# Hymba block on one core: the recursion keys turned on VectorE, one small-matmul cluster for the last Gram chunk, norms and bonus sums, and a place for each store

## The chip, the core and the metric

The kernel runs on one core of one Trainium2 chip. The metric is the device time of one execution in microseconds, as the median of several runs.

## What is computed

One layer over 512 tokens plus 16 prepended meta tokens, model width 2048, all in fp32 to the outside:

```python
hn = rmsnorm(h_res, norm_in_g)            # h_res: 16 meta tokens + 512 tokens, width 2048
P = hn @ w_in                             # 8320 columns: r, k, v, g (1024 each), 2 x 64 low rank; B, C, h, gc (1024 each)
# branch A: 16 heads of 64, RWKV-7 (r, k, v, g after a token shift)
a     = sigmoid(a0 + al @ a_lora_up); decay = exp(-exp(w_raw))
kk    = (k * k_k) / max(norm_per_head(k * k_k), 1e-12);  k = k * (1 + (a - 1) * k_a)
for t in frames:                          # state S is 64 x 64 for each head
    S = S * decay_t - (S @ kk_t) outer (kk_t * a_t) + v_t outer k_t
    y_t = S @ r_t
y_a = (groupnorm(y) + sum_per_head(r * k * r_k) * v) * silu(g)
# branch B: short gated convolution
y_b = B * causal_conv3(C * h) * silu(gc)
h_res = h_res + concat(y_a, y_b) @ w_out
out = rmsnorm(h_res)[:, 16:]
```

## The kernel before

**The projections.** The input projection is cut into 65 column tiles of 128 columns with 16 steps along the width. Each step is three matmuls in a split form of fp32: high weight x high input, high x low, low x high (L315, operands `wh`/`wl` and `xh`/`xl`). Weights arrive in transfers of 512 KB (`wr`, three buffers) and are split into a high part on ScalarE (L126) and a low part by subtraction on VectorE or POOL (L127). The tiles are named by what they give: `ps_k`, `ps_r`, `ps_v`, `ps_g`, then `ps_C`, `ps_h`, `ps_B`, `ps_gc` for the convolution. Evacuation from PSUM is on VectorE (L334); L352, L362 and L405 finish the gates and the convolution. The output projection (L1070) has the same form.

**The recurrence** is done in nine chunks of 64 frames for eight pairs of heads. `prepare(i)` builds what a pair needs, and after every second pair `invert` builds the triangular inverses of both; afterwards `recur` runs the chunks in order for all pairs. The inner matmuls are fp32, 64 rows high.

For one pair, `prepare` first makes elementwise products (`ar`, `bk`, squares `sq_h`/`sq_l`, bonus products `rk_h`/`rk_l`). TensorE then runs three clusters of its own: the *Gram cluster* (L625, chunks 0 to 7, masked into `gt` on VectorE by L635); the *second Gram cluster*, which holds chunk 8 (four records of L625) and 16 transposes of the keys (L655) that ScalarE copies into `bt` (L661, two); and the *norm cluster* (L666 and L667 the squared norms, two pieces of 288 columns each in high and low parts; L670 and L671 the bonus sums `zb`). Behind these come stores to DRAM scratch `sn` and `sg`, the stashes into the per-pair operand area `opd` (`ar`, `gt`, `bt`, `vs`, `xT`), loads `d` and `nd`, and the small block inverse on VectorE (L701 to L734; L719 and L728 are its products, whose operands have steps of 16 elements, L725 and L734 the sums; the result is `y`). `y` is stored to `sx`, loaded back in transposed places into `xT` (`load_inverse`), and `invert` goes on from there: `xn` on VectorE (L785), matmuls from L792 on, and the stash of `xT`. `recur` loads chunk operands `ct` from `opd` (L870) and runs L889 (`rz`), L906 (`u`) and the state update and outputs (L939 `zs`, L943 `zy`).

**The order of work.** TensorE's order is written by hand. The projection is a generator; `fill(ns)` draws that many ns of projection matmuls between two clusters, and `until(key)` draws until a tile is done. The table `FW` names these amounts, in ns of projection work. `later(ns, fn)` issues a DMA once that much more projection has been drawn; `run_pending` flushes what is due. All loads and stores go through SyncE's queue in program order; `tc.issue_after(state["dma"])` puts a transfer behind the latest weight load. The other engines' orders come from a scheduler with priorities; `ahead()` raises the priority of what it holds.

```python
FW = dict(
    evac=34, start=1062, lora=2200, gram=8000, gram_b=13500, gram2=4800, gram3=3500, misc=2000, v=2000, vt=1000, solve=22500, ...
...
        fill(FW["gram2"])          # second Gram cluster: chunk 8, key transposes
        fill(FW["gram3"])          # norm cluster: norms, bonus sums
        fill(FW["misc"])           # stores, block inverse
```

Of the kernel before, what the change touches and what calls it, by code (L numbers as in the profile page):

```python
# [18 lines left out]
P = 128  # L19
DM = 2048  # L20
KT = DM // P
SEQ = 512
# [18 lines left out]


FW = dict(
    evac=34, start=1062, lora=2200, gram=8000, gram_b=13500, gram2=4800, gram3=3500, misc=2000, v=2000, vt=1000, solve=22500, solve_first=26000,
    tr=3200, lev=3000, cp=4200, out=1500, begin=17000, p=2900, u=2900, s=5200, last=3700, mix=2600,
)

# [29 lines left out]
def hymba_kernel(ctx: ExitStack, tc: tile.TileContext, xt, xtok, w_in, w_out, pv, lup, cst, msk, gf, out):  # L77
# [299 lines left out]
    def use(what, i, ps):  # L377
        if what == "lora":
            use_lora(ps)
        elif what in ("k", "v"):  # L380
            t = cq.tile([P, LP], F32, tag=what, name=f"{what}{i}")
            nc.gpsimd.memset(t[:, META:CH], 0.0)
            shift_full(ps, tile_of[what] + i, f"{what}{i}", padded(t))
            got[what, i] = t
        elif what in ("r", "g"):
            t = cq.tile([P, SEQ], F32, tag=f"r{i % 2}" if what == "r" else "g", name=f"{what}{i}")
            shift_real(ps, tile_of[what] + i, f"{what}{i}", t)
            if what == "g":
                gate(t, f"r{i}")
                later(6000, lambda: nc.sync.dma_start(gated[i], t))  # L390
            got[what, i] = t
        elif what == "C":
            u = tm(f"u{i}")
            scaled(TAIL, ps, u, 14)
            got[what, i] = u
        elif what == "h":
            u = got["C", i]
            hh = tm(f"hh{i}")
            scaled(TAIL, ps, hh, 14)
            n = SEQ + 2  # L400
# [81 lines left out]
    def later(ns, fn):  # L482
        pending.append((clock[0] + ns, fn))
        pending.sort(key=lambda e: e[0])
# [81 lines left out]
    def stash(i, src, o, n, row=0, rows_n=P, c0=0, cn=NCH, step=1):  # L566
        nc.sync.dma_start(spot(i, row, rows_n, c0, cn, step, o, n), src)

    def prepare(i):
        p = i % 2  # L570
        until("k", i)
# [49 lines left out]
        bt = cq.tile([P, 2, NCH - 1, CH], F32, tag="bt", name=f"bt{i}")  # L621

        def gram(z, c, c0):
            for h, hs, ho in heads:
                nc.tensor.matmul(  # L625
# [21 lines left out]
        masked(za, 0, 4)  # L647
        masked(zc, 4, 8)
        fill(FW["gram2"])
        ze = [pi.tile([P, 1, P], F32, tag=("misc", "ser")[h], name=f"g{i}_8_{h}") for h in range(2)]  # L650
        zz = [pz.tile([P, NCH - 1, CH], F32, tag="tz", name=f"bt{i}_{h}") for h in range(2)]
        gram(ze, 8, 8)
        for c in range(NCH - 1):
            for h, hs, ho in heads:
                nc.tensor.transpose(  # L655
                    zz[h][:, c], bk[hs, c, h : h + 2, :].rearrange("p a s -> p (a s)"),
                    ident[hs, 64 * h : 64 * h + 64],
                )
        masked(ze, 8, 9)
        for h in range(2):  # L660
            nc.scalar.copy(bt[:, h], zz[h])  # L661
        fill(FW["gram3"])
        n2 = tr(f"n2{i}")
        for j, (a, b) in enumerate(((0, 288), (288, LP))):
            z = pi.tile([2, b - a], F32, tag=("misc", "ser")[j], name=f"n2_{i}_{a}")
            nc.tensor.matmul(z, ones[:, P : P + 2], sqh[:, a:b], start=True, stop=False)  # L666
            nc.tensor.matmul(z, ones[:, P : P + 2], sql[:, a:b], start=False, stop=True)  # L667
            nc.scalar.copy(n2[0:2, a:b], z)
        zb = pz.tile([P, SEQ], F32, tag="tz", name=f"zb{i}")
        nc.tensor.matmul(zb, ones[:, 0:P], rh, start=True, stop=False)  # L670
# [14 lines left out]
        nc.sync.dma_start(  # L685
            bass.AP(tensor=sn.tensor, offset=sn.offset, ap=[[CH, 2], [P, NCH], [1, CH]]), c3(n2[0:2])
        )
        for h in range(2):
            nc.sync.dma_start(rows(sg, h), gt[64 * h : 64 * h + 64, h, :, 0:CH])
        NB = 8 * NCH  # L690
        d = cq.tile([NB, 256], F32, tag="d", name=f"d{i}").rearrange("p (s t) -> p s t", t=16)
        stash(i, ar.rearrange("p c a s -> p c (a s)"), O_AR, 2 * CH)
        for h, hs, ho in heads:
            stash(i, gt[ho, h], O_KK, 2 * CH, 64 * h, 64)
            stash(i, gt[hs, h, :, CH:P], O_BR, CH, 64 * h, 64)
        nd = cq.tile([NB, 16], F32, tag="nd", name=f"nd{i}")
        nc.sync.dma_start(d, blocks(sg))
        nc.sync.dma_start(nd, sn.rearrange("(p s) -> p s", s=16))
        y = cq.tile([NB, 256], F32, tag="y", name=f"y{i}").rearrange("p (s t) -> p s t", t=16)
        nc.gpsimd.memset(y, 0.0)  # L700
        nc.vector.tensor_scalar(out=nd, in0=nd, scalar1=1e-24, scalar2=None, op0=ALU.max)  # L701
# [56 lines left out]
        nc.sync.dma_start(rbd[i], r)  # L758
        fill(FW["v"])

        vs = cq.tile([P, NCH, CH], F32, tag="vs", name=f"vs{i}")
        nc.vector.transpose(vs.rearrange("p c s -> p (c s)"), v)
        for b in range(4):
            for t in range(2):
                stash(
                    i, vs[32 * b : 32 * b + 32, :, 32 * t : 32 * t + 32], O_V + 32 * (b % 2), 32,
                    64 * (1 - b // 2) + 32 * t, 32,
                )
        fill(FW["vt"])
# [2 lines left out]
    def invert(two):  # L772
# [85 lines left out]
        for t in two:  # L858
            if t["i"] % 2 == 0:
                stash(t["i"], t["xT"], O_X, CH)  # L860
            else:
                for h, hs, ho in heads:
                    stash(t["i"], t["xT"][hs], O_X, CH, 64 - 64 * h, 64)
        fill(FW["out"] if first < NPAIR - 2 else FW["begin"])

    def load_chunk(ch, c, pairs, ops):
# [8 lines left out]
    def recur(ch):  # L875
# [4 lines left out]
        for c in range(NCH):  # L880
# [54 lines left out]
            for n in range(max(len(here), len(there))):  # L935
                if n < len(here):
                    d, j, t, o, x, a, b = here[n]
                    for h, hs, ho in heads:
                        nc.tensor.matmul(d[hs, j], t[hs, o : o + CH], x[hs], start=(a == 0), stop=(a == b - 1))  # L939
                if n < len(there):  # L940
                    d, j, x, o, t, a, b = there[n]
                    for h, hs, ho in heads:
                        nc.tensor.matmul(d[ho, j], t[hs, o : o + CH], x[hs], start=(a == 0), stop=(a == b - 1))  # L943
# [51 lines left out]
    for i in range(0, NPAIR, 2):  # L995
        invert([prepare(i), prepare(i + 1)])
    until("g", NPAIR - 1)
    ph2.close()
    with tc.tile_pool(name="ch", bufs=1, side="right", reuse_waits="tile") as ch:
        recur(ch)  # L1000
# [34 lines left out]
    for j in range(NPAIR + 4, KT):  # L1035
        while ("gc", j - NPAIR) not in ready:
            step()
        split_mix(j)
    for _ in flow:
        pass  # L1040
# [194 lines left out]
```

## Time and profile before

| | |
|---|---|
| median of 3 runs | 1056.24 us (1056.13 to 1057.02) |
| the profiled execution | 1054.6 us |
| its span, first to last instruction | 1052.8 us |
| TensorE busy | 1034.8 us (98%) |
| VectorE busy | 566.4 us (54%) |
| ScalarE, POOL busy | 365.9 us (35%), 308.3 us (29%) |
| granted TensorE clock, mean | 0.996 |

The profile is of one execution. Its rows give the start, the duration, the engine, the line, the operation with its tiles (output, then inputs), and in brackets the idle time before it with what ended that. In rows of groups, three numbers behind the count are the least, the median and the greatest duration in ns. Matmuls are pipelined: neighbours overlap, so the distance between starts is what one costs. A `x4` behind a row means that four records of one line, tile and form are drawn together.

### The profile page before, as it was taken

The page shows a single profiled execution, that of the slowest core. Times are in us where ns is not written, and L with a number is a line of the kernel's source. Part 1 is how long each engine was busy: PE and PEld are TensorE (multiplying, and loading weights), DVE is VectorE, ACT ScalarE, POOL GpSimd, SP SyncE. Part 2 cuts the span into 40 slices and gives each one's busy share as a digit, 9 for nine tenths or more (in the row PEclk, how much of TensorE's full clock was granted, in tenths as well). Part 3 has the DMA queues.
Part 4 walks back from the last instruction along what each step waited for, and adds up shares of the span by engine and source line. Part 5 has one row for each costly group of instructions (what it writes and reads, how often), then busy time and mean ns, then how long its engine had stood idle before and what let it go on. Part 6 is the DMA issues. An engine that isn't in the chain of part 4 may idle for free.

```text
span 1052.8 us, 23986 instructions
## 1 busy us (share of the span) xinstructions
PE 1034.8 (98%) x9973; PEld 945.1 (90%) x9973; DVE 566.4 (54%) x1072; ACT 365.9 (35%) x682; POOL 308.3 (29%) x315
## 2 busy tenths in 40 slices
PE   7999999999999999999999999999999999999996
PEld 6999998999998999989999989888898988888885
DVE  6774965559563658653757642455454781212132
ACT  7543422433332433233443232222222342323232
POOL 0132413324222323132323231323233242424232
PEclk9999999999999999999999999999999999999999
DMA  8446475364854363753364748778654978322314
GB/s 297 135 124 155 121 175 142 108 153 120 197 152 115 108 164 112 175 155 114 104 170 127 178 129 291 232 214 248 181 146 112 275 233 302 98 87 95 100 61 160
DMA packets 182893, 167.49 MB, mean 159 GB/s; under 512 B 120960, under 2 KB 143232, under 8 KB 182400
## 3 DMA queue, kind: packets, MB, share of 16 engines
q1 hardware_dynamic: 182208, 164.90, 53.7%
q8 instruction: 78, 1.28, 0.5%
q10 hardware_dynamic: 576, 1.07, 0.3%
q14 instruction: 31, 0.25, 0.1%
HBM read 129.05 MB, written 36.88 MB: 158 GB/s over the span
## 4 chain that ended last, share of the span: by engine, by line
PE 90%; DVE 4%; issue 2%; DMA 1%; ACT 1%; POOL 1%; SPq 0%; DVEq 0%; ACTq 0%; POOLq 0%
PE o L1070 17%; PE ps_g L315 9%; PE ps_gc L315 9%; PE ps_k L315 9%; PE ps_B L315 8%; PE ps_h L315 8%; PE ps_C L315 8%; PE ps_r L315 7%; PE ps_v L315 7%; PE g L625 2%; PE zs L939 1%; PE ps_lora L315 1%; PE rz L889 1%; PE zy L943 1%; DMA wq<-in_w_in_dram 1%
## 5 line engine op out<-in xcount | busy, mean ns | idle before, releaser
L127 POOL TENSOR_TENSOR wl<-wr,wh 128x512 fp32r<-128x512 f32 x150 | 211.2, 1410 | 456.2 <-ACT wh L126 423.2
L126 ACT CAST wh<-wr 128x512 fp32r<-128x512 f32 x312 | 188.7, 619 | 385.2 <-PE o L1070 92.2
L127 DVE TENSOR_TENSOR wl<-wr,wh 128x512 fp32r<-128x512 f32 x162 | 124.8, 775 | 241.4 <-ACT wh L126 236.0
L1070 PE MATMUL o<-wh,m 128*128 128x512 f32 (+1 forms) x484 | 145.3, 384 | 0.0
L1070 PEld LDWEIGHTS o<-wh,m 128*128 128x128 f32 x484 | 89.6, 188 | 21.3
L1070 PE MATMUL o<-wl,m 128*128 128x512 f32 (+1 forms) x242 | 92.6, 389 | 0.0
L315 PE MATMUL ps_k<-xl,wh 128*128 128x264 f32 x256 | 73.2, 286 | 0.0
L315 PE MATMUL ps_g<-xh,wl 128*128 128x258 f32 (+1 forms) x256 | 72.2, 282 | 0.9 <-DVE wl L127 0.8
L315 PE MATMUL ps_v<-xh,wh 128*128 128x264 f32 x256 | 73.1, 286 | 0.0
L315 PE MATMUL ps_k<-xh,wh 128*128 128x264 f32 x256 | 73.0, 285 | 0.0
L315 PE MATMUL ps_r<-xh,wh 128*128 128x258 f32 (+1 forms) x256 | 72.2, 282 | 0.7 <-ACT wh L225 0.7
L315 PE MATMUL ps_h<-xh,wl 128*128 128x258 f32 (+1 forms) x256 | 72.8, 285 | 0.0
L315 PE MATMUL ps_k<-xh,wl 128*128 128x264 f32 x256 | 72.7, 284 | 0.0
L315 PE MATMUL ps_v<-xh,wl 128*128 128x264 f32 x256 | 72.7, 284 | 0.0
L315 PE MATMUL ps_v<-xl,wh 128*128 128x264 f32 x256 | 72.7, 284 | 0.0
L315 PE MATMUL ps_g<-xl,wh 128*128 128x258 f32 (+1 forms) x256 | 72.4, 283 | 0.0
L315 PE MATMUL ps_h<-xh,wh 128*128 128x258 f32 (+1 forms) x256 | 72.3, 282 | 0.0
L315 PE MATMUL ps_g<-xh,wh 128*128 128x258 f32 (+1 forms) x256 | 72.3, 282 | 0.0
L315 PE MATMUL ps_C<-xh,wh 128*128 128x258 f32 (+1 forms) x256 | 72.3, 282 | 0.0
L315 PE MATMUL ps_C<-xh,wl 128*128 128x258 f32 (+1 forms) x256 | 72.3, 282 | 0.0
L315 PE MATMUL ps_r<-xl,wh 128*128 128x258 f32 (+1 forms) x256 | 72.1, 282 | 0.0
L315 PE MATMUL ps_h<-xl,wh 128*128 128x258 f32 (+1 forms) x256 | 72.1, 282 | 0.0
(271 smaller groups left out, 2705.9 us busy)
## 6 DMA issues: line engine op xcount, KB each, us to landing
wr<-in_w_in_dram SPq DMA_DIRECT2D x127, 512.0 KB
ct<-opd SPq DMA_DIRECT2D x64, 288.0 KB
wr<-in_w_out_dram SPq DMA_DIRECT2D x32, 512.0 KB
opd<-ar SPq DMA_DIRECT2D x8, 576.0 KB
opd<-gt SPq DMA_DIRECT2D x16, 288.0 KB
opd<-bt SPq DMA_DIRECT2D x32, 128.0 KB
xres<-in_xtok_dram SPq DMA_DIRECT2D x4, 768.0 KB
out_dram<-xres SPq DMA_DIRECT2D x6, 512.0 KB
```

Of the source, the lines that this page charges most:

```text
L126: nc.scalar.copy(hi, rq)
L127: eng.tensor_tensor(out=lo, in0=rq, in1=hi.bitcast(F32), op=ALU.subtract)
L315: nc.tensor.matmul(ps[r], ww[:, w], xx[:, kt, a:b], start=(kt == 0 and n == 0), stop=(kt == KT - 1 and n == 2))
L625: nc.tensor.matmul(z[h][:, c - c0], bk[hs, c, h : h + 2, :].rearrange("p a s -> p (a s)"), ar[hs, c].rearrange("p a s -> p (a s)"), start= ...
L889: nc.tensor.matmul(z[e][ho if e else hs, 0, k], t[hs, o : o + CH], t[hs, O_V : O_V + CH] if part else st[hs, 4 * e + k], start=(part == 0 ...
L939: nc.tensor.matmul(d[hs, j], t[hs, o : o + CH], x[hs], start=(a == 0), stop=(a == b - 1))
L943: nc.tensor.matmul(d[ho, j], t[hs, o : o + CH], x[hs], start=(a == 0), stop=(a == b - 1))
L1070: nc.tensor.matmul(ps[t + p], mm[:, tk], ww[:, o], start=(jj == 0 and q == 0), stop=(jj == KT - 1 and q == 2))
```

## The change

- The 16 TensorE transposes of a pair's keys and ScalarE's two copies are gone. Two VectorE transposes of 32x32 blocks (in place of L655 and L661) write `bt` instead, in a layout in which the keys of B and K alternate element by element; the stash puts it so into `opd`, in eight smaller transfers in place of four, and `recur` reads its stationary operand of `zs` with a step of two elements.
- The norm cluster's matmuls move into the second Gram cluster. The norms are cut into 512 and 64 columns in place of 288 and 288; the 64 lie in spare columns of the Gram tile. `gram3` is gone, `gram2` becomes 5500.
- Each store gets a place in the run of projection work: `sn`, `sg`, `d` and `nd` behind the latest weight load, all stashes and the stores of `rbd` and `mixd` by `later` with distances of their own, the gate's store at 14000 in place of 6000, and for odd pairs `sx` and `load_inverse` at 20500 and 22500 in place of 13500 and 16500. The stash of the inverse comes 5500 later. `run_pending` is called at two more places.

```diff
-    ... gram2=4800, gram3=3500, misc=2000, ...
+    ... gram2=5500, misc=2000, ...
-                later(6000, lambda: nc.sync.dma_start(gated[i], t))
+                later(14000, lambda: nc.sync.dma_start(gated[i], t))
-            nc.sync.dma_start(mixd[8 + i], cv)
+            later(9000, lambda: nc.sync.dma_start(mixd[8 + i], cv))
+    def behind(dst, src):
+        with tc.issue_after(state["dma"]):
+            nc.sync.dma_start(dst, src)
+    def stash_later(ns, *a):
+        later(ns, lambda: stash(*a))
...
         fill(FW["gram2"])
-        ze = [pi.tile([P, 1, P], F32, tag=("misc", "ser")[h], name=f"g{i}_8_{h}") for h in range(2)]
-        zz = [pz.tile([P, NCH - 1, CH], F32, tag="tz", name=f"bt{i}_{h}") for h in range(2)]
-        gram(ze, 8, 8)
-        for c in range(NCH - 1):
-            for h, hs, ho in heads:
-                nc.tensor.transpose(
-                    zz[h][:, c], bk[hs, c, h : h + 2, :].rearrange("p a s -> p (a s)"),
-                    ident[hs, 64 * h : 64 * h + 64],
-                )
-        masked(ze, 8, 9)
-        for h in range(2):
-            nc.scalar.copy(bt[:, h], zz[h])
-        fill(FW["gram3"])
+        ze = [pz.tile([P, P + CH], F32, tag="tz", name=f"g{i}_8_{h}") for h in range(2)]
+        gram([z[:, 0:P].unsqueeze(1) for z in ze], 8, 8)
         n2 = tr(f"n2{i}")
-        for j, (a, b) in enumerate(((0, 288), (288, LP))):
-            z = pi.tile([2, b - a], F32, tag=("misc", "ser")[j], name=f"n2_{i}_{a}")
+        zn = pi.tile([2, SEQ], F32, tag="misc", name=f"n2_{i}")
+        zs = ((zn, 0, SEQ), (ze[0][0:2, P : P + CH], SEQ, LP))
+        for z, a, b in zs:
             nc.tensor.matmul(z, ones[:, P : P + 2], sqh[:, a:b], start=True, stop=False)
             nc.tensor.matmul(z, ones[:, P : P + 2], sql[:, a:b], start=False, stop=True)
-            nc.scalar.copy(n2[0:2, a:b], z)
-        zb = pz.tile([P, SEQ], F32, tag="tz", name=f"zb{i}")
+        zb = pi.tile([P, SEQ], F32, tag="ser", name=f"zb{i}")
         ...
+        with ahead():
+            for z, a, b in zs:
+                nc.scalar.copy(n2[0:2, a:b], z)
+            masked([z[:, 0:P].unsqueeze(1) for z in ze], 8, 9)
         nc.scalar.copy(r, zb)
         fill(FW["misc"])
+        bt = cq.tile([P, NCH - 1, 2, CH // 2, 2], F32, tag="bt", name=f"bt{i}")
+        for a in range(2):
+            nc.vector.transpose(bt[:, :, :, :, a], bk[:, 0 : NCH - 1, a].rearrange("p c (t s) -> p c t s", t=2))
...
-        later(13500 if p else 29000, lambda: nc.sync.dma_start(blocks(sx), y))
-        later(16500 if p else 33000, load_inverse)
+        later(20500 if p else 29000, lambda: nc.sync.dma_start(blocks(sx), y))
+        later(22500 if p else 33000, load_inverse)
         for h, hs, ho in heads:
-            stash(i, bt[hs, h], O_B, CH, 64 * h, 64, 0, NCH - 1)
-            stash(i, bt[ho, h], O_K, CH, 64 * h, 64, 0, NCH - 1)
+            for b in range(2):
+                for t in range(2):
+                    stash_later(
+                        6500 + 1000 * (4 * h + 2 * b + t), i, bt[64 * h + 32 * b : 64 * h + 32 * b + 32, :, t].rearrange("p c s a -> p c (s a)"),
+                        O_B + 64 * b, 64, 64 * h + 32 * t, 32, 0, NCH - 1,
+                    )
...
-                        here += [(zs, j, t, O_B, u[:, e, k], 0, 2), (zs, j, t, O_K, t[:, O_V : O_V + CH], 1, 2)]
+                        bb = t[:, O_B : O_B + 2 * CH].rearrange("p (s a) -> p a s", a=2)
+                        here += [(zs, j, bb[:, 0], 0, u[:, e, k], 0, 2), (zs, j, bb[:, 1], 0, t[:, O_V : O_V + CH], 1, 2)]
```

The other stores are turned in the same manner: `ar` at 1500, `gt` at 2500 to 5500, `rbd` at 12500, `vs` at 14000 to 21000, the stash of the inverse at 5500.

More of the change, by code (lines that the diff above doesn't have):

```diff
@@ L43 @@
 FW = dict(
-    evac=34, start=1062, lora=2200, gram=8000, gram_b=13500, gram2=4800, gram3=3500, misc=2000, v=2000, vt=1000, solve=22500, solve_first=26000,
+    evac=34, start=1062, lora=2200, gram=8000, gram_b=13500, gram2=5500, misc=2000, v=2000, vt=1000, solve=22500, solve_first=26000,
     tr=3200, lev=3000, cp=4200, out=1500, begin=17000, p=2900, u=2900, s=5200, last=3700, mix=2600,
@@ L683, in blocks @@
             return bass.AP(tensor=t.tensor, offset=t.offset, ap=[[BLK, 8 * NCH], [CH, 16], [1, 16]])
-        nc.sync.dma_start(
+        behind(
             bass.AP(tensor=sn.tensor, offset=sn.offset, ap=[[CH, 2], [P, NCH], [1, CH]]), c3(n2[0:2])
@@ L688, in prepare @@
         for h in range(2):
-            nc.sync.dma_start(rows(sg, h), gt[64 * h : 64 * h + 64, h, :, 0:CH])
+            behind(rows(sg, h), gt[64 * h : 64 * h + 64, h, :, 0:CH])
         NB = 8 * NCH
         d = cq.tile([NB, 256], F32, tag="d", name=f"d{i}").rearrange("p (s t) -> p s t", t=16)
-        stash(i, ar.rearrange("p c a s -> p c (a s)"), O_AR, 2 * CH)
+        stash_later(1500, i, ar.rearrange("p c a s -> p c (a s)"), O_AR, 2 * CH)
         for h, hs, ho in heads:
-            stash(i, gt[ho, h], O_KK, 2 * CH, 64 * h, 64)
-            stash(i, gt[hs, h, :, CH:P], O_BR, CH, 64 * h, 64)
+            stash_later(2500 + 1000 * h, i, gt[ho, h], O_KK, 2 * CH, 64 * h, 64)
+            stash_later(4500 + 1000 * h, i, gt[hs, h, :, CH:P], O_BR, CH, 64 * h, 64)
         nd = cq.tile([NB, 16], F32, tag="nd", name=f"nd{i}")
-        nc.sync.dma_start(d, blocks(sg))
-        nc.sync.dma_start(nd, sn.rearrange("(p s) -> p s", s=16))
+        behind(d, blocks(sg))
+        behind(nd, sn.rearrange("(p s) -> p s", s=16))
         y = cq.tile([NB, 256], F32, tag="y", name=f"y{i}").rearrange("p (s t) -> p s t", t=16)
@@ L757, in prepare @@
         nc.vector.tensor_tensor(out=r, in0=r, in1=v[:, CH:LP], op=ALU.mult)
-        nc.sync.dma_start(rbd[i], r)
+        later(12500, lambda: nc.sync.dma_start(rbd[i], r))
         fill(FW["v"])
@@ L764, in prepare @@
             for t in range(2):
-                stash(
-                    i, vs[32 * b : 32 * b + 32, :, 32 * t : 32 * t + 32], O_V + 32 * (b % 2), 32,
+                stash_later(
+                    14000 + 1000 * (2 * b + t), i, vs[32 * b : 32 * b + 32, :, 32 * t : 32 * t + 32], O_V + 32 * (b % 2), 32,
                     64 * (1 - b // 2) + 32 * t, 32,
@@ L857, in invert, with put_inverse @@
                     nc.vector.tensor_copy(two[q]["xT"][lo, 2 - e : NCH : 2, 32:CH], z[e][lo, q])
[L858 to L863, printed above, removed]
+        def put_inverse():
+            for t in two:
+                if t["i"] % 2 == 0:
+                    stash(t["i"], t["xT"], O_X, CH)
+                else:
+                    for h, hs, ho in heads:
+                        stash(t["i"], t["xT"][hs], O_X, CH, 64 - 64 * h, 64)
+        later(5500, put_inverse)
         fill(FW["out"] if first < NPAIR - 2 else FW["begin"])
@@ L938, in recur @@
                     for h, hs, ho in heads:
-                        nc.tensor.matmul(d[hs, j], t[hs, o : o + CH], x[hs], start=(a == 0), stop=(a == b - 1))
+                        w = t[hs, o : o + CH] if o else t[hs]
+                        nc.tensor.matmul(d[hs, j], w, x[hs], start=(a == 0), stop=(a == b - 1))
                 if n < len(there):
@@ L997, in hymba_kernel @@
     until("g", NPAIR - 1)
+    run_pending(float("inf"))
     ph2.close()
@@ L1037, in hymba_kernel @@
             step()
+        run_pending(float("inf"))
         split_mix(j)
```

1 line of the change is left out of this document (removed).

## The prediction

> **What bounds the kernel now.** I read the page's busy shares and chain first, then TensorE's own waits, then timelines around the two small clusters that the change touches.
>
> ```profile
> PE 1034.8 (98%) x9973; PEld 945.1 (90%) x9973; DVE 566.4 (54%) x1072; ACT 365.9 (35%) x682; POOL 308.3 (29%) x315
> PE 90%; DVE 4%; issue 2%; DMA 1%; ACT 1%; POOL 1%; SPq 0%; DVEq 0%; ACTq 0%; POOLq 0%
> PE rz L939 <- issue: 1.6, 1, 1.6
> PE zy L943 <- issue: 1.0, 1, 1.0
> PE ps_B L315 <- DVE wl L127: 0.9, 1, 0.9
> PE ps_g L315 <- DVE wl L127: 0.8, 2, 0.4
> ```
>
> TensorE is busy for 98% of the span and carries 90% of the chain that ended last. Its waits are few and short. So the time moves only with the work in TensorE's stream, with the waits named here, and with waits that the change creates. VectorE, ScalarE and SyncE count only where one of them makes TensorE late.
>
> **Part 1: the clusters.** For each of the eight pairs the matmuls change in two places. This is the second Gram cluster of pair 0, then its norms and bonus sums:
>
> ```profile
> 82.34 0.28 PE L315 MATMUL ps_r<-xh,wh 128*128 128x258 f32 x1
> 82.55 0.49 PE L625 MATMUL g<-ar,bk 64*128 64x128 f32 x4
> 82.88 0.66 PE L655 MATMUL bt<-cs,bk 64*128 64x64 f32 x16
> 83.47 0.38 PE L315 MATMUL ps_r<-xl,wh 128*128 128x258 f32 x1
> ...
> 87.24 0.28 PE L315 MATMUL ps_r<-xh,wl 128*128 128x258 f32 x1
> 87.36 0.29 PE L666 MATMUL n<-sq_h,ones 128*2 128x288 f32 x1
> 87.88 0.40 PE L670 MATMUL zb<-rk_h,ones 128*128 128x512 f32 x1
> 88.35 0.28 PE L315 MATMUL ps_r<-xh,wh 128*128 128x256 f32 x1
> ```
>
> Matmuls overlap, so I use distances between starts. A projection matmul of this width takes 0.12 us (87.24 to 87.36). The one at 82.34 therefore ends its slot at 82.46, and the projection resumes at 83.47: the second Gram cluster costs 1.01 us. Of that, 0.09 is the change into the 64-row shape, 0.33 the four Gram records (82.55 to 82.88), and 0.59 the 16 key transposes with the way out. The norms, four matmuls of 288 columns, take 87.36 to 87.88, 0.13 each; a 512-column bonus matmul takes 0.235 ((88.35 - 87.88)/2). That makes 0.99, with no cost on the way in or out. Before: 2.00 us for a pair.
>
> After: the entry 0.09, the four records 0.33, and a way out which these rows do not separate from the transposes; 0 to 0.09 by the way in, I take 0.04. Then the norms in another cut: two of 512 columns at 0.235, two of 64 columns. No row has a 64-column matmul at full height. By width it would be 0.03 (0.13 x 64/288); the whole 0.13 is the ceiling. The weight load of this form gives a value between:
>
> ```profile
> L667 PEld LDWEIGHTS n<-sq_l,ones x16: 82/83/83, 87.4 to 577.5; 128*2 128x2 f32 x16
> ```
>
> I take 0.08, because a load of 83 ns must fit in front of each. With the bonus sums, 2 x 0.235, the cluster is 0.46 + 0.47 + 0.16 + 0.47 = 1.56 us (1.42 to 1.71). It saves 0.44 for a pair (0.29 to 0.58), and eight pairs **3.5 us (2.3 to 4.6)**. The Trainium skill ("TensorEngine Tiling (Array Packing)", Key Properties) says that changing the tiling mode drains TensorE; the 0.09 agrees in kind, and since the four Gram records remain, this change keeps that switch.
>
> **Part 2: waits that go.** In each of the groups of pairs 2/3, 4/5 and 6/7 TensorE stops once as a g tile begins:
>
> ```profile
> 255.97 0.28 PE L315 MATMUL ps_g<-xl,wh 128*128 128x258 f32 x1
> 256.64 0.39 PE L315 MATMUL ps_g<-xh,wl 128*128 128x258 f32 x1 [0.39 <-DVE wl L127]
> ...
> 408.75 0.28 PE L315 MATMUL ps_g<-xl,wh 128*128 128x258 f32 x1
> 409.41 0.39 PE L315 MATMUL ps_g<-xh,wl 128*128 128x258 f32 x1 [0.38 <-DVE wl L127]
> ...
> 561.72 0.28 PE L315 MATMUL ps_g<-xl,wh 128*128 128x258 f32 x1
> 562.14 0.39 PE L315 MATMUL ps_g<-xh,wl 128*128 128x258 f32 x1
> ...
> 254.71 0.68 DVE L734 TENSOR_REDUCE y<-prod 72x64 f32<-72x512 f32 x1
> 255.31 0.68 DVE L552 TENSOR_TENSOR rk_l<-r,rk_h 128x512 fp32r<-128x512 f32 x1
> 255.91 1.28 DVE L127 TENSOR_TENSOR wl<-wr,wh 128x512 fp32r<-128x512 f32 x2
> ```
>
> Start distances less 0.12 give 0.55, 0.54 and 0.30 us, 1.4 in all. VectorE is the reason: its weight subtraction (L127) stands behind the end of the previous pair's inverse (L734) and behind rk_l. After the change that inverse comes earlier, because the projection drawn between the second cluster and the stores shrinks from 4800 + 3500 + 2000 to 5500 + 2000 ns, 2.8 us less. The instruction order of the built kernel also has this subtraction ahead of the end of the inverse, of rk_l and of the key transposes. I count **1.4 us saved (0 to 1.4)**; what is late next there is the evacuation of the v tiles, which TensorE needs only once the next tile of that buffer begins.
>
> **Part 3: a wait that comes.** In the first group (pairs 0 and 1) VectorE's order changes for the worse. Before:
>
> ```profile
> 158.10 0.39 PE L315 MATMUL ps_B<-xl,wh 128*128 128x512 f32 x1
> 159.43 0.50 PE L315 MATMUL ps_B<-xh,wl 128*128 128x512 f32 x1 [0.94 <-DVE wl L127]
> ...
> 164.63 0.40 PE L315 MATMUL ps_gc<-xh,wh 128*128 128x512 f32 x1
> 165.10 0.40 PE L315 MATMUL ps_gc<-xh,wl 128*128 128x512 f32 x1
> ...
> 164.48 0.69 DVE L127 TENSOR_TENSOR wl<-wr,wh 128x512 fp32r<-128x512 f32 x1 [1.72 <-ACT wh L126]
> 165.09 0.68 DVE L334 TENSOR_TENSOR b<-ps_B,rs 128x512 f32<-128x512 f32 x1
> 165.69 0.70 DVE L785 STREAM_TRANSPOSE xn<-xT 128x512 f32<-128x512 f32 x1
> ```
>
> The first gc matmuls need the low halves at 165.10, 0.47 us after gc begins, and L127 made them in time. After the change b's evacuation (L334, which cannot start before the B tile ends where gc starts) stands ahead of that L127. Then b takes 0.60 (165.09 to 165.69) and L127 0.69, against 0.47: 0.8, and 0.15 for the handovers, about **0.95 us** of new wait. L127 is not always that quick: at the stop behind 158.10 two of them took 3.47 us, 1.74 each, which I put down to POOL's share of the same work running beside them.
>
> ```profile
> 157.59 3.47 DVE L127 TENSOR_TENSOR wl<-wr,wh 128x512 fp32r<-128x512 f32 x2
> ```
>
> By that the new wait would be 0.60 + 1.74 - 0.47, near 2 us. The old stop (159.43 - 158.10 - 0.235 = 1.1) stays, and may change: the same subtraction now stands behind the last steps of the inverse; I take 0.2 (-0.3 to 1). The inverse of this group is reached sooner after gc begins, since the pairs' own work moved forward against the projection, so its first transpose of x (xn, 0.70) stands behind one more subtraction: I take 0.35 (0 to 0.7). Together **1.5 us lost (0 to 4)**.
>
> **Part 4: what I count at nothing.** *Key transposes on VectorE*: two of 128x512 for a pair at the 0.70 of the xn row, 11 us in all on an engine with 46% idle. They write every second element; if that costs as in the rows below, 1.1 each and 18 us. They stand behind the weight subtractions that are due at that point. The place with the least cover is pair 2, where the first of them is ahead of ar:
>
> ```profile
> 211.42 0.69 DVE L607 TENSOR_TENSOR ar<-r,e 128x512 f32<-128x512 f32 x1
> 213.04 0.71 PE L625 MATMUL g<-ar,bk 64*128 64x128 f32 x8
> ```
>
> ar is done at 212.11, 0.93 before the Gram cluster; 0.70 fits, 1.1 makes a wait of 0.2. *ScalarE* loses two copies a pair. *Stores*: SyncE's blocking ar store waits no longer in the run of weight loads, which only adds slack to them; the eight smaller key stores replace four. *Inverse*: odd pairs load it later (22500 in place of 16500), while its use comes nearer, so its cover shrinks. By the constants and the order of the built kernel I estimate 6 to 7 us of projection between its new place and its use (L792 before), where there were 13; no row names this load as a wait of TensorE now, and I hold what is left enough. *Recursion*: the state update's stationary operand now takes every second element. The trace of before has no such load. I take nothing, bounds below.
>
> **Sum.** -3.5 - 1.4 + 1.5 = -3.4 us on 1054.6 us of the profiled execution (span 1052.8): 1051.2. The median of runs is 1056.24, 1.6 above it; the same step gives **1052.8**.
>
> **Rivals.**
> *(a) The strided weight loads slow the recursion: slower than before.*
>
> ```profile
> L939 PEld LDWEIGHTS zs<-ct x256: 135/135/135, 657.7 to 780.8; 64*64 64x64 f32 x128
> 659.43 0.28 PE L939 MATMUL zs<-ct 64*64 64x64 f32 x4
> 659.65 0.38 PE L315 MATMUL ps_h<-xh,wl 128*128 128x256 f32 x1
> L719 DVE TENSOR_TENSOR prod<-d,y x56: 156/166/1071, 101.8 to 595.9; 72x8 f32<-72x8 f32 x32, 72x64 f32<-72x64 f32 x16, 72x512 f32<-72x512 f32 x8
> L725 DVE TENSOR_REDUCE tt<-prod x56: 115/158/684, 102.0 to 597.0; 72x4 f32<-72x8 f32 x32, 72x16 f32<-72x64 f32 x16, 72x64 f32<-72x512 f32 x8
> ```
>
> The zs matmuls of the first chunk run from 657.6 to 659.65, 2.0 us for 64 with a load each. The nearest row with a step is L719, whose operand steps by 16 elements: 1.07 us where a contiguous read of the same size (L725) takes 0.68, 1.57 times as long. If the loads stretch like that and TensorE with them, eight chunks lose 8 x 2.0 x 0.57 = 9 us, up to 16 at twice. With the rest: 1062 (to 1069). It decides from 0.2 us a chunk on. For it: the loads (135 ns) are as long as the matmuls allow. Against it: the nearest strided row has a step eight times as large, and is on another engine. The Trainium skill ("SBUF — State Buffer", Door 1: The DMA port swizzle) says that SBUF is read in 16-byte lines, and that two hits on a line are enough for full speed: a step of two fp32 gives two, so by it the loads cost nothing, while L719's step gives one hit per line and pays, as its row shows. But the same sentence has each crossing to a new line pay, and this operand crosses twice as many. Chance 0.11.
>
> *(b) New waits eat the gain.* A slow L127 makes part 3 cost 3 to 4, pair 2's Gram cluster and a late inverse load add 0.2 to 1: no change, 1055 to 1057. For it: VectorE's order in the first group has no slack at all. Against it: only one of four groups has that order. Chance 0.19.
>
> *(c) The order costs nothing*, because the subtraction gets ahead: -3.5 - 1.4 = -4.9, 1051.3, on the forecast's side.
>
> **How the numbers follow.** Forecast with (c) 0.70, (b) 0.19, (a) 0.11. About 0.2% (2.1 us) is what a measurement of this kernel can tell. All of the first lies beyond it on the fast side; of (b) 0.17 is within it and 0.02 above: faster 0.70, same 0.17, slower 0.13. Low end: -4.6 - 1.4 gives 1050.2, and 0.7 less if one of the recursion's stops for issue (1.6 and 1.0 in the waits) shrinks: 1049.5. High end: 1057.5, (b) with its worst terms; (a) is left out.
>
> **What would show it.** Right: no L655, a merged cluster of about 1.5 us; no ps_g wait on L127; a wait of gc on L127 in the first group near 160 us; zs clusters still near 2.0 us in the first chunk. Wrong: zs loads over 135 ns, key transposes over 1.1 us, TensorE waiting on ar, on xn or on a chunk load.

## The result, and the profile after

The changed kernel takes 1050.93 us (median of 4 runs, 1050.09 to 1051.21) against 1056.18 for the kernel before (4 runs, 1055.93 to 1057.02): ratio 0.995, 95% interval 0.9934 to 0.9966. The profiled execution is 1051.02 us (span 1049.2), where the one before was 1054.6 (span 1052.8): 3.6 us between the two profiles, 5.25 between the medians. The forecast was 1052.8.

The page of the changed kernel, shares of busy time and the chain that ended last:

```profile
PE 1031.6 (98%) x9845; PEld 940.8 (90%) x9845; DVE 580.1 (55%) x1088; ACT 360.0 (34%) x666; POOL 311.1 (30%) x315
...
PE 94%; DMA 2%; issue 1%; DVE 1%; POOL 0%; SPq 0%; ACT 0%; DVEq 0%; ACTq 0%; POOLq 0%
```

TensorE has 128 instructions and 3.2 us of busy time less, and still bounds the kernel. Its waits (line, releaser, us in total, times, longest):

```profile
PE ps_B L315 <- DVE wl L127: 1.6, 1, 1.6
PE ps_lora L315 <- DVE xl L190: 1.5, 3, 1.0
...
PE ps_gc L315 <- DVE wl L127: 0.9, 1, 0.9
...
PE ps_h L315 <- issue: 0.6, 1, 0.6
PE t L801 <- DVE xn L794: 0.5, 1, 0.5
PE rz L902 <- DMA ct<-opd: 0.5, 1, 0.5
PE zy L958 <- issue: 0.2, 1, 0.2
```

The ps_g rows are gone. ps_B has grown, and three waits are new: gc on the subtraction, the inverse's first matmuls on xn, and the recursion's first matmuls on a chunk load. The merged cluster of pair 0 in TensorE's timeline:

```profile
83.89 0.28 PE L315 MATMUL ps_r<-xh,wh 128*128 128x258 f32 x1
84.10 0.49 PE L631 MATMUL g<-ar,bk 64*128 64x128 f32 x4
84.52 0.40 PE L663 MATMUL n<-sq_h,ones 128*2 128x512 f32 x1
84.75 0.39 PE L664 MATMUL n<-sq_l,ones 128*2 128x512 f32 x1
84.98 0.19 PE L663 MATMUL g<-sq_h,ones 128*2 128x64 f32 x1
85.01 0.19 PE L664 MATMUL g<-sq_l,ones 128*2 128x64 f32 x1
85.04 0.48 PE L666 MATMUL zb<-rk_h,ones 128*128 128x512 f32 x1
85.36 0.40 PE L667 MATMUL zb<-rk_l,ones 128*128 128x512 f32 x1
85.59 0.28 PE L315 MATMUL ps_r<-xl,wh 128*128 128x258 f32 x1
```

From the end of the slot at 84.01 to 85.59 it costs 1.58 us. The two pieces of 64 columns take 0.03 each, so the pair of them costs 0.06; the first bonus matmul takes 0.32 in place of 0.235. Its weight load of 0.19 us begins 0.03 ahead of it (85.01), where in the kernel before it began 0.13 ahead (87.75 and 87.88). I take that for the reason; it was not tested.

The first group, TensorE and then VectorE:

```profile
165.25 0.39 PE L315 MATMUL ps_gc<-xl,wh 128*128 128x512 f32 x1
166.56 0.50 PE L315 MATMUL ps_gc<-xh,wl 128*128 128x512 f32 x1 [0.92 <-DVE wl L127]
...
167.68 0.69 PE L801 MATMUL t<-xn,gt 64*64 64x64 f32 x32
168.88 0.52 PE L801 MATMUL t<-xn,gt 64*64 64x64 f32 x20 [0.50 <-DVE xn L794]
...
156.54 1.54 DVE L405 SCALAR_TENSOR_TENSOR cv<-u,pvt,cv 128x512 f32<-128x512 f32 x2 [1.25 <-ACT cv L403]
158.00 1.76 DVE L127 TENSOR_TENSOR wl<-wr,wh 128x512 fp32r<-128x512 f32 x1
165.21 0.69 DVE L334 TENSOR_TENSOR b<-ps_B,rs 128x512 f32<-128x512 f32 x1 [5.46 <-PE ps_B L315]
165.82 2.38 DVE L127 TENSOR_TENSOR wl<-wr,wh 128x512 fp32r<-128x512 f32 x2
168.12 0.70 DVE L794 STREAM_TRANSPOSE xn<-xT 128x512 f32<-128x512 f32 x1
```

VectorE is idle for 5.46 us ahead of b, then does b, the two subtractions and xn in a row while TensorE waits for the second and the fourth of them. That is the order that the prediction read from the built kernel.

### The profile page after: what moved, and what is told of

The parts are those of the page before. It is cut to its first block, busy times and chain, and to the rows that moved or that the text cites. A ratio compares the mean times of both kernels' runs of the same rounds, so it can differ in the third digit from the quotient of the medians.

```text
span 1049.2 us, 23744 instructions
## 1 busy us (share of the span) xinstructions
PE 1031.6 (98%) x9845; PEld 940.8 (90%) x9845; DVE 580.1 (55%) x1088; ACT 360.0 (34%) x666; POOL 311.1 (30%) x315
## 4 chain that ended last, share of the span: by engine, by line
PE 94%; DMA 2%; issue 1%; DVE 1%; POOL 0%; SPq 0%; ACT 0%; DVEq 0%; ACTq 0%; POOLq 0%
PE o L1087 17%; PE ps_v L315 9%; PE ps_g L315 9%; PE ps_k L315 9%; PE ps_gc L315 9%; PE ps_r L315 8%; PE ps_B L315 8%; PE ps_C L315 8%; PE ps_h L315 8%; PE g L631 2%; DMA wq<-in_w_in_dram 1%; PE zs L954 1%; PE zy L958 1%; PE ps_lora L315 1%; PE rz L902 1%
## 5 line engine op out<-in xcount | busy, mean ns | idle before, releaser
L127 POOL TENSOR_TENSOR wl<-wr,wh 128x512 fp32r<-128x512 f32 x150 | 208.8, 1392 | 460.0 <-ACT wh L126 439.6
L127 DVE TENSOR_TENSOR wl<-wr,wh 128x512 fp32r<-128x512 f32 x162 | 121.7, 756 | 224.4 <-ACT wh L126 223.2
L315 PE MATMUL ps_C<-xl,wh 128*128 128x258 f32 (+1 forms) x256 | 72.3, 282 | 0.0
L315 PE MATMUL ps_r<-xh,wl 128*128 128x258 f32 (+1 forms) x256 | 72.1, 282 | 0.0
```

The lines of the kernel that those rows point to most:

```text
L127: eng.tensor_tensor(out=lo, in0=rq, in1=hi.bitcast(F32), op=ALU.subtract)
L315: nc.tensor.matmul(ps[r], ww[:, w], xx[:, kt, a:b], start=(kt == 0 and n == 0), stop=(kt == KT - 1 and n == 2))
```

## The experiments

Each kernel was timed beside the kernel before, whose medians there were 1056.06, 1056.80 and 1057.01. Times are medians, intervals those of the ratio to the kernel before. Positions are compared at the same projection matmul of two profiles. The edits are shortened, and where an argument is given in words, the words stand for the instruction meant.

**The two kernels again.**

> The changed kernel itself, timed beside the three below and profiled a second time. Theory (the change works through TensorE's own stream): ratio 0.995 again, and in the profile the merged cluster takes 1.58 us a pair, the ps_g stops stay gone, and the first group shows its three stops near 157.8, 165.2 and 168.2 us at 1.7, 1.1 and 0.7 us. What differs between the two profiles are the stops for issue in the recursion. Rival (part of the gain is chance of one profile): the cluster or the first group's stops differ by over 0.3 us.

1051.18, ratio 0.9956 (0.9941 to 0.9971). Cluster and first group repeat (1.75, 1.08 and 0.69 us at 157.4, 164.9 and 167.8); the stop on a chunk load in the recursion was 1.38 us here.

> The kernel before, profiled a second time. Its profiled execution of 1054.6 us lay 1.6 below the median of its runs. Theory: the stops for issue in the recursion (1.80 and 1.14 us) and the start vary from run to run, and make up such a difference; clusters (2.10 us a pair) and the ps_g stops (0.55, 0.54, 0.30) repeat. Rival: the difference lies in the projection's stops, so a ps_g or ps_B stop is longer by a microsecond.

Span 1056.5, 3.7 longer than the first profile of the same kernel. TensorE's waits in this second profile of the kernel before:

```profile
PE rz L939 <- issue: 2.1, 1, 2.1
...
PE zy L943 <- issue: 1.0, 1, 1.0
...
PE ps_B L315 <- DVE wl L127: 0.9, 1, 0.9
PE ps_g L315 <- DVE wl L127: 0.8, 2, 0.4
```

The ps_g and ps_B stops repeat, as the theory said. The stops for issue stand at the same two instructions with 2.28 and 1.22 us in place of 1.80 and 1.14. A stop that I had not listed varies too: the second Gram cluster of the odd pairs waits in its middle for the mask of the first (L635) to free a bank; against the first profile it is 0.5 longer in pair 3, 0.2 in pair 5, 0.6 in pair 7. So the profile on which the prediction rests was a quick one. With 0.5 at the start that makes 2.3 us. The other 1.4 comes in one place, just behind the longer stop for issue. From 731.8 to 735.2 us the granted clock (PEclk, here the third number from the end) is 0.50, and projection matmuls start 0.21 us apart there in place of 0.12:

```profile
core 0: us, PE busy (x) PEld busy (x) DVE busy (x) ACT busy (x) POOL busy (x), PEclk, DMA share, GB/s
731.80:735.20 3.40, 3.40 (x18) 3.40 (x17) 2.24 (x6) 0.63 (x1) 0.20 (x1) 0.50 0.94 354
735.20:738.60 3.40, 3.40 (x19) 2.79 (x17) 0.43 (x1) 0.62 (x1) 2.03 (x2) 1.00 0.06 21
```

The first profile, with a stop of 1.80 us at that place, has no such stretch.

**The first group's order.**

```diff
 # i == 0 only
+with tc.issue_after(cast of B's last weight quarter):              # ScalarE
     nc.scalar.activation(cv, ...)                                  # L403
+with tc.issue_after(subtraction for B, k = 8 to 11):               # VectorE
     nc.vector.scalar_tensor_tensor(out=cv, ...)                    # L405
+with tc.issue_after(second xn):
     scaled(REAL, ps, b, META)                                      # b's evacuation, L334
...
-        with ahead():                                              # xn, L794
+        with ahead(), tc.issue_after(subtraction for gc, k = 0 to 3):
```

> The changed kernel, with edges on ScalarE and VectorE in the first group alone: the casts and subtractions of the weights go ahead of the first convolution's products, and the subtraction for gc and the transposes xn go ahead of b's evacuation. Theory: the three stops of the first group (1.75, 1.18 and 0.72 us) go or shrink under 0.3 each, so 2.5 to 3.5 us faster than the changed kernel (1047.5 to 1048.5). Rival (the stops come from late weight transfers, not from the order on the two engines): the same stops stay, no change, 1050.5 to 1051.5.

1047.50, ratio 0.9915 (0.9897 to 0.9933). All three stops are gone: between 141 and 180 us it gains 3.8 us on the changed kernel. That is the sum of the stops, 1.75, 1.08 and 0.72, and of 0.1 that the matmul behind each of the first two takes more. The theory holds: it was the order on two engines, not late transfers. For ps_B's stop the root is one step further up than the prediction had it: in the changed kernel ScalarE's L403 waited 11.8 us for POOL with four weight casts queued behind it. The three edges went in together, so what each of them is worth was not separated.

**Norms apart again.**

```diff
-    gram2=5500, misc=2000
+    gram2=4000, gram3=1500, misc=2000
         gram([z[:, 0:P].unsqueeze(1) for z in ze], 8, 8)
+        fill(FW["gram3"])                # then norms 288 + 288, bonus sums, as before
```

> The changed kernel with the norms and bonus sums in a cluster of their own again (288 and 288 columns), 1500 ns of projection behind the second Gram cluster; the total drawn stays 7500. Theory (the gain of the clusters is the 16 transposes and their way out): the two clusters cost 0.6 to 0.65 and 0.99 us, 1.6 in all against 1.58, so within 0.7 us of the changed kernel. Rival (merging saves by itself, by one switch less a pair): 0.2 to 0.4 us a pair, 1.6 to 3.2 us slower.

1049.44, ratio 0.9939 (0.9924 to 0.9954), faster than the changed kernel. The profile says why: the ps_B stop of the first group is absent (-1.6 us at 164 us) because the order came out otherwise. From 180 to 635 us, over six pairs, it loses 0.57 us, 0.09 a pair. So merging is worth 0.09, and the rest of a pair's 0.52 is the transposes and their way out: the theory, with a side effect in the first group that the expectation did not foresee.

**The pairs' work later.**

```diff
-    gram2=5500, misc=2000
+    gram2=5500, misc=4800
```

> The changed kernel with 2800 ns more projection drawn behind the merged cluster (misc 4800), so that a pair's stores and block inverse come as late against the projection as before. Theory A (the ps_g stops went because the inverse is earlier): they come back, 1.4 to 1.7 us, while the first group's stop of gc goes since the order there changes too (-1.2 to -2.5): 1049.5 to 1051.5. Theory B (they went because the subtraction stands ahead in VectorE's order): they stay gone, and the time falls by the first group alone: 1048.5 to 1050.

1048.40, ratio 0.9927 (0.9914 to 0.9939): theory B. The ps_g stops stay gone although the inverse comes as late as before; the first group's stops vanish with another order (4.2 us earlier at 181 us, 0.4 of it from the start). In their place the inverse's first matmuls wait for xn in each of the three later groups, 0.76 us each by positions:

```profile
PE t L801 <- DVE xn L794: 1.6, 3, 0.5
...
PE zy L958 <- issue: 1.3, 1, 1.3
```

**Keys contiguous.**

```diff
-        bt = cq.tile([P, NCH - 1, 2, CH // 2, 2], F32, ...)     # transposes write bt[..., a]
+        bt = cq.tile([P, NCH - 1, 2, 2, CH // 2], F32, ...)     # transposes write bt[:, :, a]
-    8 stashes of 32x8x64
+    16 stashes of 32x8x32, B and K apart; zs reads with a step of 1
```

> The changed kernel with B and K apart, as before: the key transposes write 32 elements in a row, the stash is 16 transfers of 128-byte runs in place of 8 of 256, and the stationary operand of zs has a step of one element. Theory (a step of two costs nothing): zs clusters and key transposes (0.70 us) as in the changed kernel, time within 0.7 us. Rival (the step costs): zs loads shorter than 135 ns, the recursion's clusters 0.1 us or more shorter, key transposes shorter.

1050.73, ratio 0.9947 (0.9933 to 0.9960): no difference. The key transposes take 698 ns in the median here and 703 with the interleaved write; zs loads are 135 ns in both. The first zs cluster is 2.01 us here and in the kernel before, 2.07 in the changed kernel: the step of two costs 0.05 us a chunk, 0.4 in all at most.

**A table of steps.**

```diff
+            for s in (1, 2, 4, 8):      # a line of its own each; 64 fp32 matmuls
+                nc.tensor.matmul(zs[...], ct[..., last 64*s elements, every s-th], pn[...], start=True, stop=True)
             ...                         # zs itself follows and overwrites
```

> The changed kernel with four blocks of 64 extra matmuls in each of eight chunks of the recursion, ahead of the state update, whose results are overwritten: the stationary operand has a step of 1, 2, 4 and 8 elements. Theory by two hits on a 16-byte line: steps 1 and 2 alike, about 31 ns a matmul and 2 us a block; steps 4 and 8 (one hit a line) longer, by the row of VectorE's products up to 1.6 times. Rival (weight loads of TensorE don't feel the step at all): all four blocks 2 us. Rival (each crossing pays): step 2 longer than step 1 already. With about 2 us a block the whole is 64 us longer.

1236.47. One chunk of it, steps 1, 2, 4 and 8 from above, and the loads over all chunks (least, median, greatest):

```profile
654.12 3.95 PE L953 MATMUL zs<-pn,ct 64*64 64x64 f32 x128
657.91 4.01 PE L955 MATMUL zs<-pn,ct 64*64 64x64 f32 x128
661.75 7.84 PE L957 MATMUL zs<-pn,ct 64*64 64x64 f32 x128
669.42 7.84 PE L959 MATMUL zs<-pn,ct 64*64 64x64 f32 x128
677.11 0.28 PE L965 MATMUL zs<-u,ct 64*64 64x64 f32 x4
...
L955 PEld LDWEIGHTS zs<-pn,ct x1024: 135/135/138, 657.9 to 942.3; 64*64 64x64 f32 x171
L957 PEld LDWEIGHTS zs<-pn,ct x1024: 189/213/213, 661.7 to 949.9; 64*64 64x64 f32 x171
```

The blocks take 3.78, 3.84, 7.68 and 7.68 us: steps 1 and 2 differ by 1.5%, steps 4 and 8 take twice the time, with loads of 213 ns. The Trainium skill ("SBUF — State Buffer", Door 1: The DMA port swizzle) has two hits on a 16-byte line as the condition for full speed, and for TensorE's weight loads this holds to the step. I had the length wrong: each fp32 matmul is two records, so a block is 128 records and not 64, and the price of missing lines is a factor of 2, not the 1.6 of VectorE's row.

**The old places.**

```diff
-        later(ns, lambda: stash(*a))          # and behind(), gate, rbd, mixd, sx, inverse
+        stash(*a)                             # each at once or at its old distance
```

> The changed kernel with every store and load issued where the kernel before issues it: at once, the gate's store at 6000, and sx and the inverse's load of odd pairs at 13500 and 16500. Clusters, transposes and layout stay. Theory (the places only give slack): within 1 us of the changed kernel; the first group's order on VectorE differs again, so its stops may be 1 us more or less. Rival (the places carry the gain, by stores no longer blocking the weight queue): 3 to 5 us slower than the changed kernel, 1054 to 1056.

1084.14, ratio 1.0265 (1.0247 to 1.0284): both stated sides wrong. The places do not just give slack; without them the rest of the change makes the kernel 28 us slower than before. TensorE's longest waits:

```profile
PE ps_C L315 <- DVE wl L127: 13.8, 3, 4.7
PE ps_v L315 <- POOL wl L127: 6.2, 3, 2.1
PE ps_B L315 <- ACT wh L126: 3.1, 1, 3.1
```

Not all of the loss lies in the stops themselves: at five of them the granted clock falls to 0.5, for 20.5 us in all.

Three further kernels split this. The first issues only the stashes at once, the second only the eight key stashes, the third is the kernel before with the new places alone.

```diff
 # stashes_at_once: stash_later(ns, *a) calls stash(*a) at once; all else as changed
 # keys_at_once:    as changed, but
-                    stash_later(6500 + 1000 * (4 * h + 2 * b + t), i, bt...)
+                    stash(i, bt...)
 # places_only:     the kernel before with behind(), stash_later() and every new distance
```

> The changed kernel with only the stashes of a pair (ar, gt, bt, vs) issued at once; sn, sg, d, nd, the gate, rbd, mixd, the inverse keep their new places. Theory (long runs of stash issues between two weight loads starve TensorE): most of the 33 us of the old places come back, 1070 to 1085, with stops of ps_C and ps_v on L127. Rival (it is the wait of an early store for its producer that blocks the queue, as of the gate, rbd and mixd, not the stashes): under 1056.

1068.56, ratio 1.0113 (1.0091 to 1.0135), between the two stated sides: half of the loss. Three stops of ps_C take 12.2 us; at each of them the granted clock falls to 0.5, for 6.8, 3.4 and 3.4 us, and that takes about 6 more, while the first group is 2.8 us quicker than in the changed kernel. The group of pairs 2 and 3 of this kernel, SyncE's queue first:

```profile
214.44 0.33 SPq L134 DMA_DIRECT2D wr<-in_w_in_dram  x1
...
234.97 0.88 SPq L134 DMA_DIRECT2D wr<-in_w_in_dram  x2
...
257.15 0.33 SPq L134 DMA_DIRECT2D wr<-in_w_in_dram  x1
...
265.58 2.63 SPq L567 DMA_DIRECT2D opd<-bt  x5
...
270.00 3.31 SPq L567 DMA_DIRECT2D opd<-gt  x4
...
276.66 0.41 SPq L134 DMA_DIRECT2D wr<-in_w_in_dram  x1
...
283.41 1.13 ACT L126 CAST wh<-wr 128x512 fp32r<-128x512 f32 x2
...
282.60 0.16 DVE L706 TENSOR_SCALAR nd<-nd 72x16 f32<-72x16 f32 x1
...
291.38 0.68 DVE L127 TENSOR_TENSOR wl<-wr,wh 128x512 fp32r<-128x512 f32 x1
...
287.89 0.28 PE L315 MATMUL ps_C<-xl,wh 128*128 128x258 f32 x1
292.11 0.58 PE L315 MATMUL ps_C<-xh,wl 128*128 128x258 f32 x1 [3.94 <-DVE wl L127]
```

No weight load is issued from 257.15 to 276.66, 19.5 us, while some 23 other issues go by, at about 0.5 to 0.8 us each. In the changed kernel the longest such stretch of these groups is 10.7 us. But late weights are not what stops TensorE here. Of the two halves of a weight transfer the first is subtracted on VectorE, the second on POOL; the half that TensorE waits for is cast by 284.01 (the first of ScalarE's two at 283.41), 4.0 us before TensorE stops at 288.01. Its subtraction stands in VectorE's order behind the block inverse, which begins at 282.60 (L706), and so starts at 291.38 only. In the changed kernel the same subtraction starts at 276.81 and the inverse behind it, at 277.41. The other two stops are alike, with the cast done 4.0 us ahead of each. And the stretch from 214.44 to 234.97, 20.5 us long and behind a single load too, stops nothing. In old_places the ps_C stop of this group is of the same kind (cast done at 291.78, subtraction from 299.78), the stop of ps_B is for a cast queued behind L403, which waited 18.4 us for POOL, and ps_v's stop of this group is for a POOL subtraction that took 6.6 us. So the stashes cost mainly by the order that VectorE has in this build, and the theory of starving is not borne out for these stops. Why the order comes out so was not separated.

> The changed kernel with only the eight key stashes issued at once, everything else in its new place. Theory (eight issues of 0.5 us more in a row are within the slack of three weight buffers): within 1.5 us of the changed kernel but for the first group's order, which loses its late subtraction: 1048 to 1052. Rival (the key stash waits on VectorE's transposes, and the weights behind it with it): 1056 or more, with SyncE waiting for L678.

1047.37, ratio 0.9909 (0.9892 to 0.9926), 3.8 us faster than the changed kernel. In the pairs' groups the stretches without a weight load are up to 16.9 us, and TensorE does not stop. Length does not decide: stashes_at_once has four stretches of 20.4 to 20.7 us that stop nothing, and the kernel before has one of 18.9 us (220.21 to 239.16). The gain is the first group: the order has no late subtraction, as expected, and at 178 us it is 3.7 us ahead of the changed kernel, 0.3 of it from the start. Near 641 us two waits on chunk loads (0.7 and 0.5 us), and a stretch of 3.4 us at a clock of 0.5 just behind them, take 2.2 us of this back in the profiled execution.

> The kernel before, with the new places of all stores and loads and the two flushes, and nothing else: clusters, transposes on TensorE, fills and layout stay. The run that put the old places into the changed kernel gave 1084. Theory now (places and the rest need each other: with the old places about 30 store issues stand between two weight loads, and only the kernel before has the slack for it): 1053 to 1057, little or nothing gained by the places alone. Rival (the places carry the whole gain and the transposes nothing): 1050 to 1052.

1051.73, ratio 0.9953 (0.9939 to 0.9968): the time of the whole change, with the 16 transposes still on TensorE. My theory of little or nothing falls. All TensorE waits behind the first 22 us in its profile:

```profile
PE rz L949 <- issue: 1.6, 1, 1.6
...
PE zy L953 <- issue: 1.1, 1, 1.1
```

No ps_B stop (1.09 gone against the kernel before), no ps_g stops (0.55, 0.54, 0.30), no stop in the odd pairs' second Gram cluster (0.31). The stops for issue stand at the same two instructions as in both profiles of the kernel before (1.83 and 1.24). The rival's words, that the places carry the whole gain and the transposes nothing, fall as well: see the sum below.

**The last stop.**

```diff
 # first_group_order, and:
-    run_pending(float("inf"))        # ahead of the recursion
+    run_pending(all but the store mixd of the last group)
-            later(9000, ...)         # mixd
+            later(16000 if i == 3 else 9000, ...)
```

> The kernel with the first group's order mended, and in the last group the store of the convolution's result put behind the first sixteen chunk loads of the recursion. Theory (that store waits for its product and holds ten chunk loads): TensorE's stop on a chunk load (0.6 and 0.6 us in that kernel) goes, 1.0 to 1.3 us faster than with the order alone, 1046 to 1047. Rival (the loads are limited by their own transfers): no change, 1047.5.

1045.84, ratio 0.9895 (0.9877 to 0.9913), the fastest of all. No wait on a chunk load is left, which is 1.3 us at equal positions of the two profiles; the median is 1.7 us below the order alone, in another session. It beats both kernels: 11.2 us below the kernel before by the medians of its session.

## Why the prediction was right, step by step

The time lies in the range and on the forecast side, 1.9 us below the forecast. Two of the signs that the prediction named for being wrong were there all the same: TensorE waits on xn (0.72 us, of which 0.35 was in the sum) and on a chunk load (1.03). Between the two profiles, at equal positions, the steps are

| step | forecast | measured |
|---|---|---|
| clusters, eight pairs | -3.5 | -4.2 |
| ps_g stops | -1.4 | -1.4 |
| first group: ps_B, gc, xn | +0.2, +0.95, +0.35 | +0.66, +1.08, +0.72 |
| stop in pair 5's second Gram cluster | not listed | -0.3 |
| first chunk load of the recursion | 0 | +0.7 (0.32 to 1.03) |
| stops for issue in the recursion | in the range only | -1.8 (2.94 to 1.19) |
| start, before 26 us | not listed | +0.8 (+0.4 in the second profile) |
| sum | -3.4 | -3.7 (spans: -3.6) |

That the sum comes so near is in part luck. The clusters and the stops for issue gave 2.5 us more than was put in the sum, and pair 5's stop 0.3; the first group, the chunk load and the start took 2.5 more.

**Clusters.** The mechanism was right and the saving too small by 0.08 us a pair: the way out of the transposes also delays the matmul behind the next one by 0.10, so the old clusters cost 2.10 and not 2.00. The new one cost 1.58 against 1.56, but by terms that offset each other: the 64-column pieces cost 0.06 and not 0.16, so a load of 83 ns in front of each was not the price, while the bonus sums cost 0.55 and not 0.47, and way in, records and way out 0.51 (84.01 to 84.52) and not 0.46.

**ps_g stops.** Right in size, wrong in one of its two reasons. I put the earlier inverse first and the order second. With the inverse as late as before (pairs_later) they stay gone, and the places alone remove them (places_only): it is VectorE's order, and that order follows from where the transfers stand.

**First group.** The new stop of gc was forecast at 0.95 and measured at 1.08, from a row that named the order before any run. ps_B's and xn's shares were sized too low. All of it is avoidable, as first_group_order shows.

**What I counted at nothing.** The key transposes take 0.70 us with the interleaved write, the lower of the two figures named, and no Gram cluster waited for ar. The strided weight loads are free to 1.5%, so rival (a) had the wrong price by far; the step table shows from which step it would have been right. The stores were my weakest step: "only adds slack". In the kernel before they are a gain of their own, and under the rest of the change they are a condition, since without them the time is 1084. Rival (b) named the right place, the first group, but its condition was met only in part: the first group took 2.5 us and not 3 to 4. The subtraction that held gc was quick (0.7 us); those ahead of ps_B and of xn were slow, 1.8 us each.

**What the whole gain is.** Places alone give -5.3 us by the medians, and -2.8 between the profiles, which is the sum of the five waits that are gone; the first profile of the kernel before lies 2.4 below the median of that session. On top of the places, between the profiles, the clusters give -4.2 and the shorter stops for issue -1.9 (3.07 to 1.19); the first group's three stops (1.75, 1.08, 0.72), the chunk load (1.0) and the start (0.7) take 5.2 back. That leaves -0.9, and the two profiles differ by 0.95 at the end. Two of the runs recover much of what is taken back: 1047.50 and 1045.84. That the medians moved by 5.25 and the two profiles by 3.6 is the quick first profile of the kernel before: its second one was 3.7 longer.

## What to carry to other kernels

Do not take a long stretch without a weight load for the cause of a stop that follows it: set the end of the cast and the start of the subtraction beside the stop. Here 20.5 us without a load stopped nothing, and behind 19.5 us the weights were cast 4.0 us in time while their subtraction stood behind other work. Price a stop with what follows it: behind one of 2.28 us the clock was halved for 3.4 us, which cost 1.4 more. A new order on an engine that is half idle can still cost what a removed cluster gains; look for the subtraction or copy that stands behind an evacuation which cannot start before the next tile does. And when a change has several parts, measure each part alone and the change without it: here the part that was counted at nothing carried as much as the part that was counted.

## What the runs showed of the hardware

TensorE's fp32 weight load costs the same at steps of 1 and 2 elements (blocks of 3.78 and 3.84 us) and twice as much at 4 and 8 (7.68).

Between 30 us and the end of TensorE's work the profiles have eleven stretches at a granted clock of 0.5: five in old_places, three in stashes_at_once, one each in before_again, keys_at_once and step_table. Each is 3.4 or 6.8 us long and begins between 0.8 us before and 1.2 us behind the end of a stop of TensorE. The idle time of these stops was 1.3 (in two pieces) to 4.7 us; other stops of up to 2.1 us had no such stretch, so what decides between them is open.

The stops for issue in the recursion stand at the same two instructions in three profiles of the same TensorE program, both of the kernel before and that with the places alone (1.80, 2.28, 1.83, and 1.14, 1.22, 1.24 us), and at others once the program has 128 instructions less (0.76 and 0.74 in two profiles). In the profiles of the two kernels compared here, each of these stops begins 0.1 to 2.1 us after a 16 KB transfer on the instruction queue started. Such transfers start every 4 to 10 us there, and that the instruction load is the cause of the stops was not tested.
